# Layer 0 of a two-layer trunk: both product pairs by blocks in thirteen width tiles, two of the four weight sums by accumulating transfers

## The chip, the core and the metric

The kernel runs on one core of a Trainium2 chip. The metric is the device time of one launch in microseconds. The engines are PE (TensorE), DVE (VectorE), ACT (ScalarE), POOL (GpSimd) and SP (SyncE, which here only issues transfers).

## The reference, cut to what matters

Two layers work on 512 prompt tokens and 64 sample tokens, 576 in all (`NT`). Layer 0 is a short gated convolution:

```python
b_gate, c_gate, xa, z = jnp.split(h @ w_in, 4, axis=-1)   # 1024 -> 4 x 2048
u = c_gate * xa
conv, new_buf = causal_dwconv(u, buf, conv_w)
y = b_gate * conv * jax.nn.silu(z)
return y @ w_out, new_buf
```

Layer 1 is an mLSTM block: an input projection to `xm` and `z`, a causal convolution, projections to q, k and v, a chunked recurrence over a matrix state C per head, and an output projection. Both layers start with an RMS norm, and everything is float32.

## The kernel before, in words

**Precision.** A float32 product is made of three fp32r passes. ACT casts a weight tile to `wh`, DVE subtracts to get the rest `wl`; the activations exist as `hi` and `lo`. PE then runs hi*wh, lo*wh and hi*wl.

**Layer 0 by width tiles.** The loop `for f in range(NW)` runs over sixteen tiles of 128 columns of the width 2048. Each tile has four chunks of `w_in`. Chunks 4f and 4f+1 (c gate and x, the *first pair*) end in the buffers `cx` and are computed one tile ahead. Chunks 4f+2 and 4f+3 (b gate and z, the *second pair*) are computed in their own tile; then DVE multiplies them up and splits the result `cv` for the output projection.

**A pair by blocks.** `block_pair` computes two chunks in seven products of half size (Winograd's scheme) instead of eight: each product is 12 matmuls of 128x288, so a pair takes 84 matmuls and not 96. For that the weights of the pair must first be added up. `block_weights` loads two raw tiles `r1`, `r2` of 512 KB (names `wr`), whose halves are a11, a12, a21, a22. DVE makes s1 = a21 + a22 (L297), s2 = s1 + a11 (L298), and later, by `add_up` (L337), s2 += a12 and a21 += a11. The products take a11, s1, s2, a12, a21, the new s2, and a22, in this order; each needs an ACT cast (L263) and a DVE subtract (L264) first. There are four raw buffers, so two pairs; `ws` tiles (s1, s2) come from the pool `X`; `hi`/`lo` weight pairs have four buffers.

The first pair goes by blocks in all tiles after the start. The second pair does so only where `f in SECOND`, which is tiles 3, 5, ..., 13; in the other tiles it is two plain chunks through `raw_weights` and `acc` (L215, L234).

**Order.** Small steps that may run at any time stand in a list `work`, and `run` and `drip` take some of them between products; a second list `slow` holds `query_state`, which multiplies the query by the old state C. The rest is the order of the code, and each engine runs its instructions in that order. SP's queue issues all the loads named here.

**Four places that the change also touches.** `accumulators` opens the PSUM pools; at f = 0 they are opened anew, and `mark` puts four small matmuls behind that. In layer 1, `xm` of each tile is read out of PSUM by DVE (L695). `by_token` transposes k, and its copy `kd` that POOL spreads out (L747), on PE. `query_state` uses tiles `c` of 512 KB, loaded from `cs` into two buffers.

Of the kernel before, what the change touches and what calls it, by code (L numbers as in the profile page):

```python
# [16 lines left out]
P = 128  # L17
# [38 lines left out]
LAG = 6  # L56
AHEAD = 2
FH = 2
SECOND = tuple(range(3, 14, 2))
FI = 1  # L60
EARLY = 3.45
NEARLY = 10
# [5 lines left out]
def trunk(tc, io):  # L68
    nc = tc.nc
    ctx = ExitStack()  # L70
    with ctx:
# [2 lines left out]
        const = ctx.enter_context(tc.tile_pool(name="const", bufs=1))  # L74
        small = ctx.enter_context(tc.tile_pool(name="small", bufs=2))
        accs = [None, None]
        bank_tag = ["b1"]

        def accumulators(name, blocks=None):

            for i in (1,) if blocks is None else (1, 0):
                if accs[i] is not None:
                    accs[i][0].close()
                    accs[i] = None
            for i in (0, 1) if blocks else (1,):
                stack = ctx.enter_context(ExitStack())
                accs[i] = stack, stack.enter_context(tc.tile_pool(name=f"{name}{i}", bufs=4, space=PSUM))
# [56 lines left out]
        load = nc.sync.dma_start  # L144
        store = nc.sync.dma_start
        store_act = nc.scalar.dma_start

        cols = const.tile([P, NCOL], F32, name="cols")
        cst = const.tile([P, NCST], F32, name="cst")
# [150 lines left out]

        def block_weights(c1, c2, six=False):

            groups, behind = [], []
            for i in range(1 + six):
                r1, r2 = weight_tile(), weight_tile()
                for r, c_ in ((r1, c1 + i), (r2, c2 + i)):
                    latest[0] = load(out=r, in_=io["wts"][c_]).ins
                groups.append(block_sums(r1, r2, (8, 4)[i]))
                behind = [r1, r2] if i else []
            ahead_of[c1, c2] = groups, behind  # L310

        def block_pair(c1, c2, fs, xs, out1, out2, add, mid=None, then=None, pops=0, groups=None,
                       behind=()):

            if groups is None:
                groups, behind = ahead_of.pop((c1, c2))
            a11, a12, a21, a22, s1, s2 = range(6)
            fs = [fs[0:4], fs[4:6]]  # L320
            o11, o12, o21, o22 = out1[:, 0:HT], out1[:, HT:NT], out2[:, 0:HT], out2[:, HT:NT]
            pu = X(name="pu")
            p, u = pu[:, 0:HT], pu[:, HT:NT]
            tt = nc.vector.tensor_tensor

            def product(bank_, block_, form, start):
                ws = [parts_of(g[block_]) for g in groups]
                for n, (w, g) in enumerate(zip(ws, fs)):
                    for j, forms_ in enumerate(g):
                        hi, lo = forms_[form]  # L330
                        for i, (a, x) in enumerate(((w[0], hi), (w[0], lo), (w[1], hi))):
                            nc.tensor.matmul(bank_, a[:, j, :], x, start=(start and n + j + i == 0),  # L332
                                             stop=(n == len(groups) - 1 and j == len(g) - 1 and i == 2), skip_group_check=True)

            def add_up(out, block_):
                for g in groups:
                    tt(g[out], g[out], g[block_], ALU.add)  # L337

            bx = block("p1")
            product(bx, a11, "b11", True)  # L340
            by = block("p6")
            nc.scalar.activation(by, bx, AF.Copy, scale=-1.0)  # L342
            run(pops)
            bw = block("p5")
            product(bw, s1, "t1", True)
            m5 = X(HT, name="m5")
            nc.scalar.copy(m5, bw)
            run(pops)
            product(by, s2, "t2", False)
            nc.scalar.copy(u, by)  # L350
            add_up(s2, a12)
            product(bx, a12, "b21", False)
            add_up(a21, a11)
            run(pops)
            if pops:
                drip()
            product(by, a21, "t3", False)
            if xs is None or add:
                nc.scalar.copy(p, by)
            else:  # L360
                bv = block("p7")
                nc.scalar.copy(bv, by)
            product(bw, s2, "b22", False)
            run(pops)
            product(by, a22, "t4", False)
            run(pops)
            mid = list(mid or ())
            for go in mid[0:2]:
                go()
            wx = [parts_of(r[:, 4:8, :]) for r in behind]  # L370
            if then:
                block_weights(*then)
            if add:
                tt(p, p, m5, ALU.subtract)
                tt(o22, o22, p, ALU.add)
                tt(o12, o12, u, ALU.subtract)
                tt(o12, o12, bw, ALU.add)
                tt(o11, o11, bx, ALU.add)
                tt(o21, o21, by, ALU.add)
                return  # L380
            if xs is None:
                tt(o22, p, m5, ALU.subtract)
                nc.scalar.copy(o11, bx)
                tt(o12, bw, u, ALU.subtract)
                nc.scalar.copy(o21, by)
                return
            plain(bx, bw, c1 + 1, xs, None, wx[0:1])
            nc.scalar.copy(o11, bx)
            if mid:
                nc.scalar.copy(o12, bw)  # L390
            tt(o12, o12 if mid else bw, u, ALU.subtract)
            for go in mid[2:3]:
                go()
            if pops:
                drip()
            plain(by, bv, c2 + 1, xs, None, wx[1:2])
            nc.scalar.copy(o21, by)
            if mid:
                nc.scalar.copy(o22, bv)
            tt(o22, o22 if mid else bv, m5, ALU.subtract)  # L400
            for go in mid[3:]:
                go()
# [115 lines left out]
                ins = nc.tensor.matmul(b[:, 0:256], warm[:, 0:128], warm, start=True, stop=True).ins  # L518
            return ins

        accumulators("acc0", False)
        load_buffers("raw", "raw0", 4)
        load_buffers("C", "scratch0")
        layer0[0] = True
# [65 lines left out]
        for f in range(NW):  # L590
# [24 lines left out]
            if f == 0:  # L615
                for i in range(2):
                    acc = mm("acc")
                    products(acc, weights(4 + i), h1, True, True)
                    nc.scalar.copy(cx[i], flat(acc))
                    if i:  # L620
                        block_weights(8, 9)
                    first_blocks(2 + i)
                accumulators("acc0a", True)
                bank_tag[0] = "blk"
                mark(h1[0][0][:, 0:P], h1[0][0][:, 0:HT])
            elif f + 1 < NW:
                block_pair(4 * f + 4, 4 * f + 5, fs, None, *cx, False, pops=1)
# [55 lines left out]
        for f in range(NW):  # L683
# [4 lines left out]
            if f < 2:  # L688
                u = raws[f]
                nc.vector.tensor_tensor(u, u, rb, ALU.mult)  # L690
            else:
                acc = gemm(80 + f, 1, h2)
                u = T(name="xm")
                if f < NW - 2:
                    nc.vector.tensor_tensor(u, flat(acc), rb, ALU.mult)  # L695
                else:
                    nc.scalar.copy(u, flat(acc))
                    nc.vector.tensor_tensor(u, u, rb, ALU.mult)
# [45 lines left out]
        def spread(t, dup):  # L744

            for u in range(2):
                nc.gpsimd.tensor_copy(  # L747
                    dup[:, 128 * u:128 * u + 128].rearrange("p (g s t) -> p g s t", g=4, s=4),
                    t[:, NP + 32 * u:NP + 32 * u + 32].rearrange("p (g t) -> p g t", t=8)
                    .unsqueeze(2).broadcast_to([P, 4, 4, 8]))  # L750
# [140 lines left out]
                h2.append(split(xs[m]))  # L891

        h2 = []
        heads = [dict(h=h, kt=[], qt=[], kd=[], qp=[]) for h in range(NH)]
        order = [4 * h + dt for h in (3, 0, 1, 2) for dt in range(4)]
        for h in (3, 0, 1, 2):
            st = heads[h]
            for dt in range(4):
# [19 lines left out]
                if dt % 2 == 0:  # L918
                    st["kd"].append(T(512, name="kd"))
                dup = st["kd"][-1][:, 256 * (dt % 2):256 * (dt % 2) + 256]  # L920
                spread(k, dup)
                work.append(lambda k=k, dup=dup, h=h, dt=dt: by_token(
                    k, dup, KSCALE, kps[h][dt].rearrange("p (i d) -> p i d", d=128),
                    kss[h][:, :, 128 * dt:128 * dt + 128]))
# [12 lines left out]
            work.append(lambda h=h, t=st["qt"]: gates(8 + h, t))  # L937
            if h == 2:
                break
            work.extend(lambda st=st, dt=dt: scores(st, dt) for dt in range(4))  # L940
            work.extend(lambda st=st, u=u: sample_scores(st, u) for u in range(2))
            if h in (3, 0, 1):
                slow.extend(lambda h=h, i=i: query_state(heads[h], unit(h, *divmod(i, 4)), i) for i in range(8))

        accumulators("acc2", False)
        load_buffers("raw", "raw2", 2)
# [651 lines left out]
def _arrays(a):  # L1598
# [5 lines left out]
    kq = np.stack([_chunks(f["b_w_k"][0]), _chunks(f["b_w_q"][0])], 1)  # L1604
    wts = np.concatenate([t.reshape(-1, P, KD, P) for t in (
        ain, _chunks(f["a_w_out"][0]), bin_[:NW], _chunks(f["b_w_v"][0]), kq, bin_[NW:], _chunks(f["b_w_out"][0]))], 0)
    cols = np.zeros((P, NCOL), np.float32)

    def put(name, v):
# [80 lines left out]
```

## Time and profile before

| | |
|---|---|
| median of 3 runs | 1685.6 us (1679.59 to 1689.01) |
| profiled execution, its own time | 1681.13 us |
| its span, granted TensorE clock | 1679.3 us, 0.992 |
| PE busy | 1646.1 us, 98% |
| DVE busy | 1121.8 us, 67% |
| ACT busy | 780.1 us, 46% |
| POOL busy | 106.8 us, 6% |
| loads `wr` from `wts` | 222 of 512 KB, 3.6 us from issue to landing (median) |

A line of a view names the line of the kernel, the engine, the operation and the tiles, output first. `x2` is the number of instructions put together in a row. In square brackets stands the idle time of the engine just ahead of the row, and who ended it. A row's duration overlaps the next one by some hundredths where an engine is pipelined, so what an instruction costs in a full queue is read from start to start.

### The profile page before, as it was taken

The numbers are of one execution on the slowest core, as the hardware profiler recorded it, in microseconds if no ns is written. First come the engines' busy times: TensorE is split into PE (matmuls) and PEld (weight loads), VectorE is DVE, ScalarE is ACT, GpSimd is POOL, SyncE is SP. The second block draws the span as 40 slices with busy tenths as digits, with TensorE's granted clock in tenths as the row PEclk, the third lists the DMA queues.
The fourth block names the chain that finished last, engine by engine and source line by source line (L and its number), as shares of the span: only waits on it lengthen the run. The fifth ranks groups of instructions, "written<-read, shape, count | busy, mean of one in ns | idle before, by whom it ended". The sixth has DMA issues, their size and how long they took to land. (4 is left out here: it accounts for less than half of the span.)

```text
span 1679.3 us, 31080 instructions
## 1 busy us (share of the span) xinstructions
PE 1646.1 (98%) x12161; PEld 1568.7 (93%) x12161; DVE 1121.8 (67%) x2108; ACT 780.1 (46%) x1546; POOL 106.8 (6%) x241
## 2 busy tenths in 40 slices
PE   9999999999999999999899999999999998999998
PEld 8999999999999999999899989889888887989998
DVE  7988888874336985655956456446458658588775
ACT  5555555543233554434644334344445446556431
POOL 0000000000000000000201010010102000000000
PEclk9999999999999999999999999999999899999999
DMA  5222223233332434535534455454556577998992
GB/s 197 73 94 94 93 93 105 92 101 127 121 122 89 136 123 142 156 116 167 158 101 136 149 176 170 135 172 161 176 182 237 188 239 261 335 332 303 371 332 105
DMA packets 109794, 279.57 MB, mean 166 GB/s; under 512 B 11312, under 2 KB 33712, under 8 KB 109648
## 3 DMA queue, kind: packets, MB, share of 16 engines
q1 hardware_dynamic: 94288, 260.27, 46.4%
q10 hardware_dynamic: 15360, 17.32, 3.0%
q8 instruction: 95, 1.56, 0.4%
q14 instruction: 51, 0.42, 0.1%
HBM read 213.89 MB, written 63.66 MB: 165 GB/s over the span
## 5 line engine op out<-in xcount | busy, mean ns | idle before, releaser
L332 PE MATMUL p<-hi,wh 128*128 128x288 f32 x1316 | 389.0, 297 | 1.2 <-ACT p L342 1.2
L332 PE MATMUL p<-lo,wh 128*128 128x288 f32 x1316 | 386.9, 295 | 0.0
L332 PE MATMUL p<-hi,wl 128*128 128x288 f32 x1316 | 385.9, 295 | 0.0
L234 PE MATMUL acc<-hi,wh 128*128 128x256 f32 (+1 forms) x1328 | 288.5, 298 | 2.1 <-DVE xm L695 1.6
L234 PE MATMUL acc<-lo,wh 128*128 128x256 f32 (+1 forms) x1328 | 287.6, 297 | 0.0
L234 PE MATMUL acc<-hi,wl 128*128 128x256 f32 (+1 forms) x1328 | 287.2, 297 | 0.0
L332 PEld LDWEIGHTS p<-hi,wh 128*128 128x128 f32 x1316 | 246.5, 188 | 14.3 <-issue 3.8
L263 ACT CAST wh<-wr 128x256 fp32r<-128x256 f32 (+1 forms) x266 | 152.0, 572 | 225.4 <-PE p L332 127.1
L332 PEld LDWEIGHTS p<-lo,wh 128*128 128x128 f32 x1316 | 247.1, 188 | 0.0
L332 PEld LDWEIGHTS p<-hi,wl 128*128 128x128 f32 x1316 | 246.3, 188 | 0.0
L214 ACT CAST wh<-wr 128x512 fp32r<-128x512 f32 x202 | 124.8, 620 | 235.9 <-PE acc L234 176.6
L264 DVE TENSOR_TENSOR wl<-wr,wh 128x256 fp32r<-128x256 f32 (+1 forms) x266 | 163.2, 628 | 103.3 <-ACT wh L263 100.2
L234 PEld LDWEIGHTS acc<-hi,wh 128*128 128x128 f32 x1328 | 223.8, 190 | 7.5 <-issue 3.5
L234 PEld LDWEIGHTS acc<-hi,wl 128*128 128x128 f32 x1328 | 223.3, 190 | 1.6 <-issue 1.3
L234 PEld LDWEIGHTS acc<-lo,wh 128*128 128x128 f32 x1328 | 223.3, 190 | 0.5 <-issue 0.2
L215 DVE TENSOR_TENSOR wl<-wr,wh 128x512 fp32r<-128x512 f32 x202 | 138.5, 687 | 110.5 <-ACT wh L214 102.2
L263 ACT CAST wh<-ws 128x512 fp32r<-128x512 f32 (+1 forms) x177 | 99.8, 566 | 205.5 <-PE p L332 112.5
L264 DVE TENSOR_TENSOR wl<-ws,wh 128x512 fp32r<-128x512 f32 (+1 forms) x177 | 108.8, 620 | 58.5 <-ACT wh L263 58.0
L417 PE MATMUL p<-hi,wh 128*128 128x288 f32 x496 | 109.6, 299 | 0.0
L417 PE MATMUL p<-hi,wl 128*128 128x288 f32 x496 | 108.2, 296 | 0.0
L1210 DVE SCALAR_TENSOR_TENSOR c<-c,cols,r 128x512 f32<-128x512 f32 x128 | 91.1, 741 | 23.7 <-PE r L1209 21.2
L417 PE MATMUL p<-lo,wh 128*128 128x288 f32 x496 | 106.9, 295 | 0.0
(382 smaller groups left out, 2572.8 us busy)
## 6 DMA issues: line engine op xcount, KB each, us to landing
wr<-wts SPq DMA_DIRECT2D x222, 512.0 KB, 3.6
c<-cs SPq DMA_DIRECT2D x112, 512.0 KB, 5.9
cs_out<-c SPq DMA_DIRECT2D x64, 512.0 KB, 6.9
x<-xcs SPq DMA_DIRECT2D x20, 288.0 KB, 4.6
x<-xT SPq DMA_DIRECT2D x16, 288.0 KB, 4.1
xcs<-xc ACTq DMA_DIRECT2D x16, 288.0 KB, 2.4
ld<-xcs SPq DMA_DIRECT2D x16, 288.0 KB, 8.6
cp_out<-cp ACTq DMA_DIRECT2D x16, 257.0 KB, 7.5
```

The source lines that it names most:

```text
L214: last_act[0] = nc.scalar.copy(hi, raw[:, 4 * i:4 * i + 4, :]).ins
L215: nc.vector.tensor_tensor(lo, raw[:, 4 * i:4 * i + 4, :], hi.bitcast(F32), ALU.subtract)
L234: nc.tensor.matmul(acc[:, o:o + j - i], a[:, k % 4, :], x[:, i:j], start=(first and k == 0 and p == 0), stop=(last and k == 7 and p == 2))
L263: last_act[0] = nc.scalar.copy(hi, src).ins
L264: nc.vector.tensor_tensor(lo, src, hi.bitcast(F32), ALU.subtract)
L332: nc.tensor.matmul(bank_, a[:, j, :], x, start=(start and n + j + i == 0), stop=(n == len(groups) - 1 and j == len(g) - 1 and i == 2), ski ...
L417: nc.tensor.matmul(b, a[:, k % 4, :], x[:, t:t + HT], start=bool(start) and k == 0 and i == 0, stop=(k == n - 1 and i == 2), skip_group_ch ...
L1210: ins = nc.vector.scalar_tensor_tensor(ct[:, j, :], ct[:, j, :], dec[:, o + j:o + j + 1], r, ALU.mult, ALU.add).ins
```

## The change

The set of tiles whose second pair goes by blocks becomes 2 to 14. In layer 0 two of the four sums of a pair are made by transfers: s1 is loaded from DRAM once more as a21 (256 KB, SP), a transfer issued by POOL adds a22 to it from DRAM, and another adds a11 to a21 in place. DVE keeps s2 = s1 + a11 and s2 += a12. The host stores the chunks concerned with their eight slices permuted. Beside this come four small edits: the PSUM pools of layer 0 are opened in the block form from the start; `xm` of tile 2 of layer 1 goes through a copy by ACT; two empty items stand in `work` ahead of the first `by_token`; and the state tiles `c` are asked for one unit ahead (`meet`).

```diff
-SECOND = tuple(range(3, 14, 2))
+SECOND = tuple(range(2, 15))
...
+        add_load = nc.gpsimd.dma_start
...
         def block_weights(c1, c2, six=False):
 
+            if layer0[0]:
+
+                r1, r2 = weight_tile(), weight_tile()
+                for r, c_ in ((r1, c1), (r2, c2)):
+                    latest[0] = load(out=r, in_=io["wts"][c_]).ins
+                a11, a12, a21, a22 = [r[:, i:i + 4, :] for r in (r1, r2) for i in (0, 4)]
+                s1, s2 = [X(512, name="ws").rearrange("p (k x) -> p k x", x=P) for _ in range(2)]
+                load(out=s1, in_=io["wts"][c2][:, 0:4, :])
+                add_load(out=s1, in_=io["wts"][c2][:, 4:8, :], accum_op=ALU.add)
+                add_load(out=a21, in_=io["wts"][c1][:, 0:4, :], accum_op=ALU.add)
+                nc.vector.tensor_tensor(s2, s1, a11, ALU.add)
+                ahead_of[c1, c2] = [(a11, a12, a21, a22, s1, s2)], []
+                return
...
             add_up(s2, a12)
             product(bx, a12, "b21", False)
-            add_up(a21, a11)
+            if not layer0[0]:
+                add_up(a21, a11)
...
-        accumulators("acc0", False)
+        accumulators("acc0", True)
...
-                accumulators("acc0a", True)
-                bank_tag[0] = "blk"
                 mark(h1[0][0][:, 0:P], h1[0][0][:, 0:HT])
...
-                if f < NW - 2:
+                if 2 < f < NW - 2:
                     nc.vector.tensor_tensor(u, flat(acc), rb, ALU.mult)
...
+        def meet(h, i):
+
+            query_state(heads[h], waiting.pop(), i)
+            n = met.index((h, i)) + 1
+            if n < len(met):
+                waiting.append(unit(met[n][0], *divmod(met[n][1], 4)))
...
+                if (h, dt) == (3, 0):
+                    work.extend([lambda: None] * 2)
...
-                slow.extend(lambda h=h, i=i: query_state(heads[h], unit(h, *divmod(i, 4)), i) for i in range(8))
+                slow.extend(lambda h=h, i=i: meet(h, i) for i in range(8))
...
+    blk = [c for c in range(8, 64) if c % 4 < 2 or c // 4 in SECOND]
+    wts[blk] = wts[blk][:, :, [0, 2, 4, 6, 1, 3, 5, 7]]
```

Over the whole program PE's listing shrinks by 84 matmuls, and POOL's grows by the 54 accumulating transfers of 27 pairs.

DVE before, in an odd tile: the second sum of one pair, then a21 += a11 of the same pair, then the subtracts of the pair ahead of it. Here `wr254`, `wr255` are r1, r2 of the later pair, and `wr239`, `wr240` of the earlier one; `ws` are s1 and s2.

```order
L298 TENSOR_TENSOR ws257_1837<-ws256_1836,wr254_1832 128x512
L337 TENSOR_TENSOR wr255_1833<-wr255_1833,wr254_1832 128x4x128
L264 TENSOR_TENSOR wl267_1886<-ws242_1704,wh267_1885 128x512
L337 TENSOR_TENSOR ws242_1704<-ws242_1704,wr239_1699 128x512
L648 TENSOR_TENSOR cv222_1555<-acc247_1767,cv222_1555 128x576
L264 TENSOR_TENSOR wl268_1904<-wr239_1699,wh268_1903 128x512
L649 TENSOR_TENSOR cv222_1555<-cv222_1555,z243_1707 128x576
L264 TENSOR_TENSOR wl269_1923<-wr240_1700,wh269_1922 128x512
```

DVE after, about one tile: the subtract two rows ahead of the first shown here is the last reader of `wr232`, whose buffer `wr272` takes over; the last row is s2 of the pair that is loaded there, and it needs the accumulated `ws274`.

```order
L265 TENSOR_TENSOR wl265_1811<-wr233_1578,wh265_1810 128x512
L613 TENSOR_TENSOR cx236_1587<-cx236_1587,rb281_505 128x576
L618 TENSOR_TENSOR cv231_1576<-cv231_1576,rb70_470 128x576
L265 TENSOR_TENSOR wl266_1828<-ws235_1582,wh266_1827 128x512
L265 TENSOR_TENSOR wl267_1844<-wr233_1578,wh267_1843 128x512
L265 TENSOR_TENSOR wl280_1888<-wr250_1725,wh280_1887 128x512
L265 TENSOR_TENSOR wl283_1909<-ws252_1729,wh283_1908 128x512
L397 TENSOR_TENSOR b255_1736<-pu256_1737,m5262_1774 128x288
L399 TENSOR_TENSOR z254_1735<-p5260_1757,pu256_1737 128x288
L265 TENSOR_TENSOR wl285_1929<-ws253_1730,wh285_1928 128x512
L659 TENSOR_TENSOR z254_1735<-z254_1735,rb70_470 128x576
L314 TENSOR_TENSOR ws275_1878<-ws274_1877,wr272_1873 128x512
```

Two sums are gone from DVE, and the one that is left (L314) now stands behind two transfers in a row instead of one load.

The queues that feed it. SP after, at the same place (a load of r1, the load of s1 behind it, then r2):

```order
L308 DMA wr272_1873<-wts 128x1024
L311 DMA ws274_1877<-wts 128x512
L308 DMA wr273_1874<-wts 128x1024
L308 DMA wr290_2021<-wts 128x1024
L311 DMA ws292_2025<-wts 128x512
L308 DMA wr291_2022<-wts 128x1024
```

POOL after, at the same place; before, its listing has only the `cpa` copies here:

```order
L312 DMA ws252_1729<-wts 128x512
L617 COPY cpa_507<-u230_1575 128x2
L313 DMA wr251_1726<-wts 128x512
L312 DMA ws274_1877<-wts 128x512
L313 DMA wr273_1874<-wts 128x512
L312 DMA ws292_2025<-wts 128x512
L617 COPY cpa_507<-u270_1871 128x2
L313 DMA wr291_2022<-wts 128x512
```

Two transfers per pair have come onto POOL, in one order with its copies.

PE at the first `by_token`, before (tb is the transpose of the copy kd):

```order
L332 MATMUL p61266_9895<-hi1228_9673,wl1292_10027 128x288
L332 MATMUL p11308_10079<-hl1287_9986,wh1310_10084 128x288
L758 MATMUL tb1313_10109<-cst_70,kd1300_10063 128x128 x2
L332 MATMUL p11308_10079<-hl1287_9986,wh1310_10084 128x288
L332 MATMUL p11308_10079<-hl1287_9986,wl1310_10085 128x288
```

and after:

```order
L346 MATMUL p61329_10045<-hi1291_9823,wl1355_10177 128x288
L346 MATMUL p11371_10229<-hl1350_10136,wh1373_10234 128x288
L771 MATMUL tb1384_10345<-cst_70,kd1363_10213 128x128 x2
L346 MATMUL p11371_10229<-hl1350_10136,wh1373_10234 128x288
L346 MATMUL p11371_10229<-hl1350_10136,wl1373_10235 128x288
```

The transposes stand between the same two matmuls in both, 84 rows earlier in the listing of after, which is as many as the matmuls that went in layer 0.

More of the change, by code (lines that the diff above doesn't have):

```diff
@@ L76, in trunk @@
         accs = [None, None]
-        bank_tag = ["b1"]
+        bank_tag = ["blk"]
         def accumulators(name, blocks=None):
@@ L893, in trunk @@
         h2 = []
+        met = [(h, i) for h in FAR for i in range(8)]
+        waiting = []
+        def meet(h, i):
[3 more added lines that the diff above has]
+                waiting.append(unit(met[n][0], *divmod(met[n][1], 4)))
         heads = [dict(h=h, kt=[], qt=[], kd=[], qp=[]) for h in range(NH)]
@@ L939, in trunk @@
                 break
+            if h == 3:
+                waiting.append(unit(3, 0, 0))
             work.extend(lambda st=st, dt=dt: scores(st, dt) for dt in range(4))
```

## The prediction

> **What bounds the kernel now.** I read the busy shares of the page first, then layer 0 by stretches of two tiles, then PE's waits in the timeline.
>
> ```profile
> PE 1646.1 (98%) x12161; PEld 1568.7 (93%) x12161; DVE 1121.8 (67%) x2108; ACT 780.1 (46%) x1546; POOL 106.8 (6%) x241
> 97.00:143.00 46.00, 46.00 (x349) 46.00 (x349) 38.64 (x68) 24.68 (x49) 1.16 (x2) 1.00 0.32 100
> 189.00:235.00 46.00, 46.00 (x349) 46.00 (x349) 38.91 (x68) 24.62 (x49) 1.17 (x2) 1.00 0.30 99
> 327.00:373.00 46.00, 46.00 (x349) 46.00 (x348) 35.38 (x61) 24.55 (x50) 1.17 (x2) 1.00 0.31 95
> ```
>
> PE is the bound, 98% of the span. The columns of the lower three rows are start and end, length, and the busy time of PE, weight loads, DVE, ACT and POOL, then the granted clock and the share of the transfer engines. In layer 0 PE has no gap: 46.00 of 46.00. So every matmul taken out there is worth its full time, as long as nothing else becomes late. DVE is the nearest, some 39 of 46; ACT has 25.
>
> PE's waits that the four small edits address:
>
> ```profile
> 50.64 0.80 PE L407 MATMUL mark<-hi 128*128 128x288 f32 x4 [1.61 <-ACT cx L619]
> 520.94 0.50 PE L234 MATMUL acc<-hi,wh 128*128 128x256 f32 x2 [1.64 <-DVE xm L695]
> 838.06 0.56 PE L758 MATMUL tb<-cst,kd 128*128 128x128 f32 x2 [3.11 <-POOL kd L747]
> 1003.34 1.07 PE L845 MATMUL qa<-c,qp 128*32 128x512 f32 x8 [0.91 <-DMA c<-cs]
> 1123.03 1.06 PE L845 MATMUL qa<-c,qp 128*32 128x512 f32 x8 [1.05 <-DMA c<-cs]
> 1242.50 1.07 PE L845 MATMUL qa<-c,qp 128*32 128x512 f32 x8 [0.87 <-DMA c<-cs]
> ```
>
> Together 9.2 us. The brackets hold the idle time ahead of the row.
>
> **The matmuls that go.** Seven tiles (2, 4, ..., 14) change from 96 to 84 matmuls in the second pair, so 84 go. What one takes in a full queue:
>
> ```profile
> 1613.27 3.99 PE acc L234 x30
> ```
>
> That is 0.133 us; the stretches above give 46.00/349 = 0.132. 84 x 0.133 = 11.1 us, all on the bound.
>
> **DVE's load.** Its prices are starts in a queue without gaps:
>
> ```profile
> 243.04 0.75 DVE L496 SCALAR_TENSOR_TENSOR cv<-u,cols,cv 128x511 f32<-128x511 f32 x1
> 243.71 0.28 DVE L498 SCALAR_TENSOR_TENSOR cv<-ext,cols,cv 128x64 f32<-128x64 f32 x1
> 243.90 0.68 DVE L264 TENSOR_TENSOR wl<-wr,wh 128x512 fp32r<-128x512 f32 x1
> 244.50 0.74 DVE L496 SCALAR_TENSOR_TENSOR cv<-u,cols,cv 128x510 f32<-128x510 f32 x1
> ```
>
> A 128x512 operation costs 0.60 (243.90 to 244.50), one of 510 to 576 columns 0.67, one of 64 columns 0.19, and one of 288 columns by scale about 0.37. In after, a tile has 14 subtracts and 4 sums (10.8), nine wide operations (6.0), four of 288 (1.5) and the small ones (0.5): 18.8 us. PE's tile becomes 46.15/2 - 0.8 = 22.28 us (two tiles are 348 matmuls now, 336 then, at 0.1326). So DVE stands at 84%. With the four sums that the transfers take over it would be 21.2, 95%. ACT gets three more casts in the even tiles, some 2 us of its 21 idle in 46, and stays clear. The load on DVE alone costs nothing.
>
> **The accumulating transfers.** This is the unknown: no transfer issued by POOL, and none that adds, is in the trace. What it must meet follows from the order. The buffer of r1 comes free at DVE's last subtract on it. Then SP loads r1, s1 behind it, POOL's transfer adds a22, and only then may DVE run s2 (L314). DVE runs in order, so what stands behind L314 waits too: the subtracts for the earlier pair, and with them PE. The rows of the loads:
>
> ```profile
> wr<-wts SPq DMA_DIRECT2D x59, 512.0 KB, 3.5
> DMA to landing us min/median/max: 3.3/3.6/4.8
> 261.55 0.33 SPq L307 DMA_DIRECT2D wr<-wts  x1
> ```
>
> A load of 512 KB takes 3.6 us, and an issue on SP 0.33 us. The s1 load, issued 0.4 behind r1, lands about 0.4 + 3.6 = 4.0 after the subtract that freed the buffer (an estimate; I give 256 KB no discount, since it shares the engines with r1). If the accumulate takes A, s2 may run L = 4.0 + A after that subtract. Between the two DVE has twelve operations, 6.6 us (6.3 for the other kind of pair). A longer L is a stall, once for each pair, twice a tile: DVE then needs 18.8 + 2L - 12.9 per tile, and 0.3 for the gap behind a dependent operation. That meets 22.28 at L = 8.0, so at **A = 4.0 us**. Beyond that each us of A costs 2 us a tile, over tiles 2 to 10 some 18 us, less about 3 us that the prepared weights (two products of twelve matmuls, 1.6 us each) cover once. From tile 11 `cx` shares the pool of `ws`, and the loads come later; I add nothing for it.
>
> What is A? The nearest rows are other transfers of about that size:
>
> ```profile
> xcs<-xc ACTq DMA_DIRECT2D x16, 288.0 KB, 2.4
> cp_out<-cp ACTq DMA_DIRECT2D x16, 257.0 KB, 7.5
> ```
>
> The quickest is 2.4 us, a busy one 7.5; both ends go into the range. An addition reads two tiles of 256 KB, as many bytes as one `wr` load, and I take that row: 3.6 us. It is 0.4 us inside the limit, so I charge nothing, with little left. At 2.4 nothing either; at 7.5 it is 18 x 3.5 - 3 = 60 us. The second accumulate (a21, L313) is needed only at the fifth product, four products or 6.4 us of PE later than s1; it hides behind these. POOL's `cpa` copies (1.17 us in 46) stand in the same queue, but u is done well before.
>
> The Trainium skill, DMA: Bandwidth & Descriptors, "Anatomy of one DMA — SWDGE (gpsimd) path", fits a transfer issued by GpSimd with 2.0 us plus its bytes over 436 GB/s; an estimate by it is 2.6 us for 256 KB, which no run here shows for an adding one. By it L would be 6.6, no wait at all, and the sum the same.
>
> At the start L314 of the first pair stands ahead of the weight subtracts for the first tile:
>
> ```profile
> 22.35 1.29 DVE L215 TENSOR_TENSOR wl<-wr,wh 128x512 fp32r<-128x512 f32 x2
> ```
>
> DVE comes there at 22.35, r1 has landed by about 21.8 (its load is issued at 18.0 in before, plus 3.8), and s1 is loaded ahead of it. Between no wait and 2 us; I take nothing, since PE has weights ahead.
>
> **The four waits.** *mark*: nothing is moved and the reopening, which waits for the last `cx`, goes; the weights of the first products are cast before. 1.6 us. *xm*: the read-out goes from DVE to ACT, where it stands behind these:
>
> ```profile
> 518.54 0.67 ACT L165 CAST hi<-xm 128x576 fp32r<-128x576 f32 x1
> 519.13 0.62 ACT L214 CAST wh<-wr 128x512 fp32r<-128x512 f32 x1
> 520.05 1.41 DVE L695 TENSOR_TENSOR xm<-acc,rb 128x576 f32<-128x576 f32 x2
> ```
>
> ACT's copy runs from about 519.7 to 520.4, where the first of DVE's two ended at about 520.75. PE gains 0.4 of 1.64, between 0 and 1.6. *c*: the groups of `qa` that waited stood 25 rows of PE behind the one before; in after the closest are 37 rows apart, and in before groups 37 and 38 rows apart did not wait. 2.8 us, between 0 and 2.8. *kd*: the transposes did not move on PE, and the copies that they wait for are on POOL as before:
>
> ```profile
> 830.74 7.49 POOL L747 COPY kd<-k 128x128 f32<-128x128 f32 x2 [22.92 <-issue]
> ```
>
> Two copies of 128x128 take 7.49 us there. I take nothing, between 0 and 3.1: the two empty items do not do what they look like.
>
> **The sum.** 11.1 + 1.6 + 0.4 + 2.8 = 15.9 us. From the profiled execution, 1681.1, that is 1665.2. The median of the runs is 4.5 above the profiled one; the forecast for a median is 1685.6 - 15.9 = 1669.7, 1670, with a range of its own of 1664 to 1676.
>
> **The rivals.**
> *The accumulates are late (slower).* A over 5.5 us makes L314 the place where DVE stands, and PE runs out of weights twice a tile. At A = 6 the loss is 18 x 2 - 3 = 33, the time 1685.6 - 15.9 + 33 = 1703. For it: the 7.5 of `cp_out`, and the addition runs beside the 512 KB load of r2, issued meanwhile. It decides from A = (15.9 + 8.4 + 3)/18 + 4 = 5.5. Against it: layer 0 uses only 0.30 of the transfer engines. A second way to the same: DVE shuts POOL out while it works, as the 7.49 us for two `kd` copies suggest, and POOL cannot issue in time.
> The Trainium skill, SBUF — State Buffer, "Who interferes with whom", says that POOL's transfers get their descriptors late while DVE runs operations that use two ports, such as copies; a tensor_tensor with two inputs in SBUF contends only with what GpSimd reads. The `kd` row agrees with the latter part. No run here shows the former.
> *Gains and stalls cancel.* A between 4.6 and 5.5 costs 8 to 24 us: within 8.4 us of before, about 1686 at A = 5.1.
> *All four waits go.* If POOL's `kd` copies happen to run in a freer stretch, 3.1 more: 1666.6.
>
> **How the numbers follow.** No change that can be told is within 0.5%, 8.4 us. Chances: forecast (A up to 4.6, where the loss is under 8 us) 0.50, all four waits 0.07, cancelling 0.17, late 0.26. Faster 0.57, same 0.17, slower 0.26. The range starts at 1660, the four-wait case less the scatter of the runs (6 us below the median), and ends at 1705, A of about 6.2 (18 x 2.2 - 3 = 37, 1706); some 0.15 lies above, 0.03 below.
>
> **What the profile of after would show.** Right: a tile of 22.3 us in layer 0, PE 46 of 46 there, L314 with waits of under 1.5 us each, `mark` and the three `qa` without their waits, `kd` still near 3 us, `xm` near 1.2. Wrong: DVE idle ahead of L314 for 3 us and more, released by POOL's transfer, and PE idle ahead of `p` for `wl` in each tile. The median landing of the `ws` accumulate tells A: 4.0 is the limit.

## The result: slower by 0.66%

| | before | after |
|---|---|---|
| median of 7 runs | 1684.77 us | 1696.69 us |
| ratio, 95% interval | | 1.0066 (1.0049 to 1.0084) |
| profiled execution, own time | 1681.13 us | 1696.83 us |
| its span, clock | 1679.3 us, 0.992 | 1695.0 us, 0.988 |

Forecast was 1670 with 0.57 for faster; what came is the place and the mechanism of the rival *the accumulates are late*, at 0.26, but not its condition: it asked for an accumulate of over 5.5 us, and the median here is 4.4. The ratio says some 11 us more; the two profiled executions stand 15.7 apart, since that of before is one of its quickest runs.

Layer 0 after, in stretches of two tiles; the columns are start and end, length, busy time of PE, weight loads, DVE, ACT and POOL, the clock and the share of the transfer engines:

```profile
97.00:143.00 46.00, 43.33 (x317) 41.86 (x316) 37.67 (x67) 26.30 (x55) 7.13 (x9) 1.00 0.63 155
143.00:189.00 46.00, 40.43 (x297) 39.26 (x296) 33.13 (x61) 25.43 (x53) 7.36 (x10) 1.00 0.60 144
189.00:235.00 46.00, 45.39 (x326) 44.45 (x325) 36.81 (x64) 27.13 (x56) 7.57 (x10) 0.96 0.64 161
327.00:373.00 46.00, 44.28 (x327) 43.12 (x326) 36.19 (x66) 26.82 (x57) 8.15 (x10) 1.00 0.64 154
```

PE, which had 46.00 of 46.00 and 349 matmuls, now has gaps and runs 297 to 327. DVE is not full, it stands: 33 to 38 us. The transfer engines went from 0.30 to 0.62. What ended the longest waits of DVE and of PE in layer 0 (us, times, longest):

```profile
DVE ws L314 <- DMA ws<-wts: 49.3, 24, 4.1
PE p L346 <- DVE wl L265: 14.8, 14, 3.0
```

DVE waits at L314 for the transfer that adds, 24 times for 2.05 us, and PE waits for the `wl` that stand behind. One such pair, SP's rows first, then POOL, DVE and PE:

```profile
151.43 0.33 SPq L308 DMA_DIRECT2D wr<-wts  x1
151.81 0.43 SPq L311 DMA_DIRECT2D ws<-wts  x1
156.41 0.89 POOL L312 DMA_DIRECT2D ws<-wts  x1 [8.70 <-DVE u L614]
160.87 0.69 DVE L314 TENSOR_TENSOR ws<-ws,wr 128x512 f32<-128x512 f32 x1 [2.60 <-DMA ws<-wts]
162.22 0.40 PE L346 MATMUL p<-hi,wl 128*128 128x288 f32 x1 [2.01 <-DVE wl L265]
```

From the issue of r1 to s2 are 9.44 us: 0.38 to the issue of s1, 4.60 to the issue of the accumulate, 4.46 to s2. (The releaser in POOL's bracket is not the last one: the u it names was long there; it is the landing of s1.) The transfers after, KB each, median us to landing:

```profile
ws<-wts SPq DMA_DIRECT2D x27, 256.0 KB, 3.9
ws<-wts POOLq DMA_DIRECT2D x27, 256.0 KB, 4.4
wr<-wts POOLq DMA_DIRECT2D x27, 256.0 KB, 4.0
```

How much layer 0 lost is read from one line of each kernel, the first and the last start of the product that ends a tile (count, duration, first and last start). Before, then after:

```profile
L649 DVE TENSOR_TENSOR cv<-cv,z x16: 750/750/759, 64.5 to 390.2; 128x576 f32<-128x576 f32 x16
L662 DVE TENSOR_TENSOR cv<-cv,z x16: 747/750/758, 63.5 to 405.0; 128x576 f32<-128x576 f32 x16
```

14.8 us later where 11.1 less were due. Against the kernel *s2 written later* (below), which has the same transfers and no such loss, it is 27.3 us. Not all of that is idle time: after two of PE's longest waits, of 3.01 and 2.25 us, the granted clock fell for a while (the column before the last two):

```profile
188.00:192.00 4.00, 4.00 (x21) 4.00 (x21) 4.00 (x9) 0.62 (x1) 0.00 (x0) 0.61 0.20 18
260.00:264.00 4.00, 3.20 (x13) 3.20 (x14) 4.00 (x9) 0.62 (x1) 0.00 (x0) 0.57 0.25 44
```

There the matmuls start 0.24 us apart and not 0.13. Added up from start to start, some 17 us of the loss lie in fourteen waits of PE, some 3 in these two slow stretches, and some 7 in many starts that are a few tenths late. The four small waits, where they are now, after:

```profile
48.12 0.69 PE L422 MATMUL mark<-hi 128*128 128x288 f32 x4
534.49 0.53 PE L235 MATMUL acc<-hi,wh 128*128 128x256 f32 x2 [1.04 <-ACT xm L710]
839.37 0.40 PE L346 MATMUL p<-hi,wh 128*128 128x288 f32 x1 [2.80 <-ACT p L356]
846.57 1.25 POOL L760 COPY kd<-k 128x128 f32<-128x128 f32 x2 [25.16 <-issue]
```

`mark` and the `qa` no longer wait. The wait for `kd` is not there, but a little ahead of it PE now waits 2.80 for another step, and after that the two `kd` copies took 1.25 us and not 7.49.

### The profile page after: what moved, and what is told of

Read it like the earlier page. It is cut to its first block, busy times and chain, and to the rows that moved or that the text cites. A ratio compares the mean times of both kernels' runs of the same rounds, so it can differ in the third digit from the quotient of the medians.

```text
span 1695.0 us, 31248 instructions
## 1 busy us (share of the span) xinstructions
PE 1650.9 (97%) x12077; PEld 1564.0 (92%) x12077; DVE 1118.6 (66%) x2117; ACT 802.8 (47%) x1610; POOL 148.0 (9%) x295
## 5 line engine op out<-in xcount | busy, mean ns | idle before, releaser
L346 PE MATMUL p<-hi,wl 128*128 128x288 f32 x1512 | 446.7, 298 | 15.1 <-DVE wl L265 14.8
L346 PE MATMUL p<-hi,wh 128*128 128x288 f32 x1512 | 448.4, 298 | 4.2 <-ACT p L356 2.8
L346 PE MATMUL p<-lo,wh 128*128 128x288 f32 x1512 | 446.4, 296 | 0.0
L264 ACT CAST wh<-wr 128x512 fp32r<-128x512 f32 (+1 forms) x294 | 169.5, 576 | 210.4 <-PE p L346 120.7
L235 PE MATMUL acc<-hi,wh 128*128 128x256 f32 (+1 forms) x1104 | 240.2, 298 | 2.1 <-ACT xm L710 1.0
L265 DVE TENSOR_TENSOR wl<-wr,wh 128x512 fp32r<-128x512 f32 (+1 forms) x294 | 180.2, 632 | 89.5 <-ACT wh L264 88.8
L235 PE MATMUL acc<-hi,wl 128*128 128x256 f32 (+1 forms) x1104 | 239.0, 297 | 0.0
L235 PE MATMUL acc<-lo,wh 128*128 128x256 f32 (+1 forms) x1104 | 238.3, 297 | 0.0
L264 ACT CAST wh<-ws 128x512 fp32r<-128x512 f32 x198 | 112.7, 570 | 225.9 <-PE p L346 123.4
L265 DVE TENSOR_TENSOR wl<-ws,wh 128x512 fp32r<-128x512 f32 x198 | 122.7, 625 | 51.0 <-ACT wh L264 50.6
L432 PE MATMUL p<-hi,wh 128*128 128x288 f32 x496 | 109.2, 300 | 0.0
L432 PE MATMUL p<-hi,wl 128*128 128x288 f32 x496 | 107.3, 295 | 0.0
L432 PE MATMUL p<-lo,wh 128*128 128x288 f32 x496 | 107.0, 295 | 0.0
```

What stands on the lines that cost most here:

```text
L235: nc.tensor.matmul(acc[:, o:o + j - i], a[:, k % 4, :], x[:, i:j], start=(first and k == 0 and p == 0), stop=(last and k == 7 and p == 2))
L264: last_act[0] = nc.scalar.copy(hi, src).ins
L265: nc.vector.tensor_tensor(lo, src, hi.bitcast(F32), ALU.subtract)
L432: nc.tensor.matmul(b, a[:, k % 4, :], x[:, t:t + HT], start=bool(start) and k == 0 and i == 0, stop=(k == n - 1 and i == 2), skip_group_ch ...
```

## The experiments

The theory after the result: what costs is where s2 stands in DVE's order, twelve operations behind the subtract that frees the raw buffer, while load, load and accumulate take 9.4 us. The rivals: the traffic of the transfers or POOL's part in it; DVE or the raw buffers being unfit for blocks in both pairs; the small edits. All ratios are to the kernel before.

| kernel | ratio (95%) | last `cv<-cv,z` |
|---|---|---|
| after | 1.0066 (1.0049 to 1.0084) | 405.0 |
| small edits alone | 0.9991 (0.9980 to 1.0001) | 390.3 |
| four sums on DVE | 0.9913 (0.9894 to 0.9931) | 378.4 |
| a21 alone by transfer | 0.9918 (0.9900 to 0.9936) | 379.5 |
| s1 alone by transfers | 1.0033 (1.0021 to 1.0045) | 398.0 |
| s1 asked for earlier | 1.0008 (0.9996 to 1.0021) | 395.2 |
| s2 written later | 0.9906 (0.9887 to 0.9926) | 377.7 |
| transfer copies, does not add | 0.9966 (0.9954 to 0.9977) | 384.6 |
| four sums, kd on DVE | 0.9904 (0.9887 to 0.9920) | 377.9 |
| before with tiles 2 to 14 | 0.9960 (0.9943 to 0.9978) | 378.5 |
| after with tiles 3, 5, ..., 13 | 1.0017 (1.0001 to 1.0033) | 393.1 |

### The small edits alone

```diff
# before, with the four small edits only
-        accumulators("acc0", False)
+        accumulators("acc0", True)
...
```

> The kernel before with the four small edits alone; products and sums as before. Theory (the loss of the change lies in layer 0 alone, at the sum that waits for an accumulate): all that PE no longer waits for at mark (1.6), kd (3.1), the three qa (2.8) and part of xm (0.6) is gained, 8.1 us, ratio 0.995, and layer 0 stays without a gap in PE. Rival (part of the loss comes from these edits, for instance from what moved behind kd or the earlier loads of c): ratio 1.000 or more, with new waits of PE after 600 us.

0.9991 and not 0.995: most of the 8 us did not come. `mark` comes 1.0 us earlier, but eight microseconds on PE waits for the next late step, and the wait for `kd` stayed, as the order had it (the kernel's own rows):

```profile
57.30 0.40 PE L332 MATMUL p<-hi,wh 128*128 128x288 f32 x1 [0.61 <-ACT m L347]
PE tb L756 <- POOL kd L745: 3.1, 1, 3.1
```

The last `cv<-cv,z` is where it was, 390.3. From the first `qa` to the first `r` PE needs 390.6 us and not 394.0, and 390.6 to 390.8 in every later kernel with that edit: 3.4 us. With `xm`, 0.6, that makes 4; the ratio holds 0 to 3.4. Most of the difference is the clock. After the wait for `kd` the granted clock was 0.55 from 836 to 840 us and 0.60 from 840 to 844 in this profiled execution, and 1.00 after the same wait in that of before. From the first `r` to the end, which these edits don't touch, before took 366.0 us and this kernel 373.6 (the others 367.5 to 374.0). The trace has half the clock for some 27 us of that in before and for some 40 here, which by estimate is 6.6 of the 7.6 us. Over all executions of this experiment the mean granted clock was 0.989 here and 0.991 in before, which is some 3 us of 1683. Why it is lower is not shown.

### Four sums on DVE

```diff
-                load(out=s1, in_=io["wts"][c2][:, 0:4, :])
-                add_load(out=s1, in_=io["wts"][c2][:, 4:8, :], accum_op=ALU.add)
-                add_load(out=a21, in_=io["wts"][c1][:, 0:4, :], accum_op=ALU.add)
+                nc.vector.tensor_tensor(s1, a21, a22, ALU.add)
...
-            if not layer0[0]:
-                add_up(a21, a11)
+            add_up(a21, a11)
```

> The changed kernel with all four weight sums on DVE again, no accumulating transfer: both pairs by blocks in tiles 2 to 14. Theory (only the wait for the accumulate costs): DVE has 21.2 us of work in a tile of 22.28, PE stays without gaps in layer 0, 84 matmuls less are worth 11.1 us and the waits 8.1: ratio 0.9886, some 1666 us. Rival A (DVE was full, so that the transfers were needed): 95 per cent plus gaps for dependent operations is more than PE's tile, PE loses 0.5 to 1 us a tile, 6 to 13 us, ratio 0.992 to 0.996. Rival B (four raw buffers cannot feed seven half products in both pairs, whoever adds): about as slow as the changed kernel, 1.005.

0.9913. The same stretch of two tiles as above:

```profile
143.00:189.00 46.00, 46.00 (x350) 46.00 (x349) 44.69 (x80) 29.19 (x61) 1.17 (x2) 1.00 0.31 92
```

DVE is at 44.69 of 46 and PE has no gap. Rivals A and B fall: DVE at 97% by its rows feeds PE, and the accumulating transfers were not needed. The 0.9886 of the theory is missed all the same, because it counted 8.1 us for the small edits. Blocks in both pairs are worth 378.4 against 390.2 us, 11.8.

### One sum by transfer

```diff
# a21 alone: s1 made by DVE
-                load(out=s1, in_=io["wts"][c2][:, 0:4, :])
-                add_load(out=s1, in_=io["wts"][c2][:, 4:8, :], accum_op=ALU.add)
+                nc.vector.tensor_tensor(s1, a21, a22, ALU.add)
```

> The changed kernel with only the sum a21 += a11 made by a transfer; s1 is made by DVE from the two loaded tiles. Theory: the chain of load, load and accumulate ahead of s2 is gone, the other accumulate is needed four products later and hides; DVE 20.0 of 22.28; no gap in PE: ratio 0.9886 as with four sums, or better than these if DVE is short there. Rival (any accumulating transfer, by its traffic or by POOL, slows the loads or DVE): between 0.995 and 1.006.

```diff
# s1 alone: a21 += a11 made by DVE
-                add_load(out=a21, in_=io["wts"][c1][:, 0:4, :], accum_op=ALU.add)
...
-            if not layer0[0]:
-                add_up(a21, a11)
+            add_up(a21, a11)
```

> The changed kernel with only s1 made by transfers; a21 += a11 is DVE's again. Theory: the chain ahead of s2 is as long as in the changed kernel, about 9.5 us from the load of r1 to s2, and DVE has 0.6 us more in a tile: as slow as the changed kernel or slower, ratio 1.006 to 1.012. Rival (the traffic of the transfers): half of the accumulates are gone, half of the loss of 28 us goes, ratio about 0.998.

0.9918 and 1.0033. An accumulate that nobody waits for early is free: with a21 alone PE is at 46.00 and the transfer engines at 0.46. With s1 alone, at the same 0.46, PE loses again:

```profile
143.00:189.00 46.00, 46.00 (x350) 46.00 (x349) 42.60 (x75) 29.75 (x62) 4.63 (x7) 1.00 0.46 115
143.00:189.00 46.00, 42.79 (x313) 41.39 (x312) 37.29 (x67) 25.01 (x53) 4.30 (x6) 1.00 0.46 124
```

The traffic is the same in both, and only one loses, so it isn't the traffic. With s1 alone the loss is smaller than the theory said: 1.0033 lies between its 1.006 and the rival's 0.998, and against four sums on DVE layer 0 loses 19.6 us (398.0 against 378.4) where after loses 26.6. Two things differ. The accumulate is somewhat quicker without the one on a21 beside it, 4.0 us and not 4.3 (median between 100 and 300 us). And with a21 += a11 on DVE again mostly 12 or 13 of its operations stand between the issue of r1 and s2, and not 10 or 11. How much of the 7 us belongs to each is not shown.

### s1 asked for earlier

```diff
+                n = turns.index(c1) + 1
+                if n < EARLY_SUMS:
+                    early[turns[n]] = first_sum(turns[n] + 1, T)
                 nc.vector.tensor_tensor(s2, s1, a11, ALU.add)
```

(`first_sum` holds the load of s1 and the accumulate, `turns` the order of the pairs.)

> The changed kernel, but the load of s1 and the accumulate on it are asked for one pair ahead, into tiles of another pool, for the first eighteen of 27 pairs; the same transfers and the same sums. Theory (DVE stands at s2 because r1's free buffer, the load of s1 and the accumulate follow one another, 9.5 us): the accumulate has landed before r1 has, s2 waits for r1 alone, under 1 us; of the 28 us that PE loses in layer 0 the 23 or so of these tiles go: ratio 0.991 to 0.994. Rival (the traffic of the transfers, or POOL's work, slows DVE, ACT or the loads): the same transfers, ratio still 1.004 to 1.008.

1.0008, a miss of both. Where it did what it should, between 97 and 235 us, PE is nearly whole; at the start, and from where the early asking ends, it is not:

```profile
51.00:97.00 46.00, 42.39 (x312) 41.19 (x311) 35.95 (x65) 22.97 (x46) 6.28 (x9) 1.00 0.53 131
97.00:143.00 46.00, 45.31 (x341) 44.84 (x340) 38.82 (x68) 28.46 (x59) 8.17 (x10) 1.00 0.68 170
143.00:189.00 46.00, 45.59 (x345) 45.35 (x344) 38.95 (x69) 28.63 (x59) 8.17 (x10) 1.00 0.66 163
235.00:281.00 46.00, 42.60 (x318) 41.90 (x317) 37.69 (x67) 27.02 (x57) 6.94 (x9) 1.00 0.56 135
```

The rows that do well have the most traffic, 0.66 to 0.68, which speaks against the rival again. But s2 also moved in DVE's order: in one pair of two it stands 3 to 5 operations behind the issue of r1, in the other 18 to 22. So this run moves two things.

### s2 written later

```diff
-                nc.vector.tensor_tensor(s2, s1, a11, ALU.add)
                 ahead_of[c1, c2] = [(a11, a12, a21, a22, s1, s2)], []
...
             product(bx, a11, "b11", True)
+            if layer0[0]:
+                for g in groups:
+                    tt(g[s2], g[s1], g[a11], ALU.add)
```

> The changed kernel with one line moved: s2 = s1 + a11 is written behind the first product of its own pair and not where the pair is loaded, so that on DVE it stands some eighteen operations behind the subtract that frees the buffer (10.5 us) and not twelve (6.6). Theory (the chain is as long as before, but what costs is DVE's order): the chain of 9.5 us fits, DVE does not stand, ratio 0.991 to 0.994. Rival A (the transfers as such): 1.004 to 1.008. Rival B (s2 now comes too late for the third product): the wait turns up on PE ahead of p, ratio above 1.

0.9906. This is the run that decides: every transfer of the changed kernel is in it, two for each pair on POOL, and the whole loss is gone. One pair, SP, POOL and DVE (L356 is s2 here):

```profile
154.23 0.33 SPq L308 DMA_DIRECT2D wr<-wts  x1
154.61 0.43 SPq L311 DMA_DIRECT2D ws<-wts  x1
159.10 0.86 POOL L312 DMA_DIRECT2D ws<-wts  x1 [7.22 <-DMA ws<-wts]
167.88 0.68 DVE L356 TENSOR_TENSOR ws<-ws,wr 128x512 f32<-128x512 f32 x1
143.00:189.00 46.00, 46.00 (x350) 46.00 (x349) 40.17 (x71) 29.69 (x62) 7.53 (x10) 1.00 0.71 166
```

s2 comes 13.65 us after the issue of r1 and waits for nothing. The accumulate is even slower than in after (4.7 us against 4.3, same stretch), the transfer engines are at 0.71, and PE is whole.

### The addition priced

```diff
-                add_load(out=s1, in_=io["wts"][c2][:, 4:8, :], accum_op=ALU.add)
+                add_load(out=s1, in_=io["wts"][c2][:, 4:8, :])
```

> The changed kernel with the transfer on s1 copying a22 over it and not adding it (so s1 leaves a21 out); every instruction and every wait stands as in the changed kernel. It prices the addition: Theory (what counts is the chain, with its fixed parts): issue to landing 4.0 to 4.4 us as with the addition, the time within 0.2 per cent of the changed kernel, ratio 1.006. Rival (the addition, which must read what it adds to, is what makes the transfer slow): 2.4 to 3.4 us, the chain 1 to 2 us shorter, 18 us less for each: ratio 0.985 to 0.996.

0.9966: the rival is right here. A plain copy by the same queue lands after 3.3 us (median between 100 and 300 us), the addition takes 4.3. (s1 then lacks a21; the kernel leaves that sum out.) The order of every engine is that of after, so this is a measured dose: the chain from the issue of r1 to s2 takes 8.68 us and not 9.44 (medians between 90 and 295 us), and the last `cv<-cv,z` comes 20.4 us earlier (384.6 against 405.0). The forecast's price, 18 us for each microsecond, was for tiles 2 to 10. These tiles take 14.8 us less here for 0.76 us of chain, and some 3 of the 14.8 are the two slow stretches of after, which this run does not have: 16 to 19 us for each.

```profile
145.49 0.33 SPq L308 DMA_DIRECT2D wr<-wts  x1
150.39 0.55 POOL L312 DMA_DIRECT2D ws<-wts  x1 [7.58 <-DVE u L614]
153.73 0.69 DVE L314 TENSOR_TENSOR ws<-ws,wr 128x512 f32<-128x512 f32 x1 [1.40 <-DMA ws<-wts]
```

### kd on DVE

```diff
# four sums on DVE, and
-                spread(k, dup)
-                if (h, dt) == (3, 0):
-                    work.extend([lambda: None] * 2)
+                spread(k, dup, nc.vector.tensor_copy if (h, dt) == (3, 0) else nc.gpsimd.tensor_copy)
```

> The variant with four sums on DVE, and the two copies kd of the first by_token on DVE instead of POOL, without the two empty items. Theory: the two copies took 7.49 us on POOL while DVE was busy and PE waited 3.1 us for them; on DVE they take some 0.4 and the wait goes: 0.9913 - 0.0018 = 0.9895. Rival (another wait is next, as behind mark): 0.991.

0.9904 against 0.9913: the intervals overlap, so the 3 us are not shown by the times. In the trace the wait for `kd` is gone and from the first `tb` to the first `qa` PE needs 293.7 us, where the variant with four sums alone needs 295.8. With *s2 written later* it is the quickest of the study, 16 us under before.

### The parts of the change by themselves

```diff
# before
-SECOND = tuple(range(3, 14, 2))
+SECOND = tuple(range(2, 15))
```

> The kernel before with the set of tiles whose second pair goes by blocks set to 2 to 14, and nothing else: four sums on DVE, the four small edits undone. Theory: 84 matmuls less at 0.1327 us are 11.1 us, all on the bound, and layer 0 stays without gaps: ratio 0.9934. The difference to the variant with four sums and the small edits (0.9913) is what these are worth, some 3 us, not 9. Rival (DVE's 95 per cent needs the start that the edit at mark gives): 0.996 or more.

0.9960, the rival's number, and the theory's 0.9934 lies outside the interval; but the rival's reason is not it: in layer 0 the whole gain is there (378.5 against 390.2, 11.7 us). It is given back later. The three `qa` waits, 2.8 us in before, are

```profile
PE qa L845 <- DMA c<-cs: 5.9, 3, 3.8
```

in the profiled execution, one of them 3.8, and from the first `qa` to the first `r` PE needs 399.4 us and not 394.0. Of these 5.4 us 3.1 are the waits; after the one of 3.8 the granted clock was 0.50 between 1113 and 1118 us. In these two profiles, then, the edit on `c` is worth more beside the blocks than alone.

```diff
# after
-SECOND = tuple(range(2, 15))
+SECOND = tuple(range(3, 14, 2))
```

> The changed kernel with the set of tiles as before (3, 5, ..., 13), so that the even tiles run two plain chunks between the pairs; transfers and small edits as in the changed kernel, 20 pairs instead of 27. Theory: the chain of some 9.5 us is met by more DVE and PE work between two pairs, and DVE has 34 us of work in 46 plus some 9 of standing: PE loses under 3 us, ratio 0.998 to 1.002 (the small edits alone gave 0.9991). Rival (each accumulated pair costs about 1 us whatever the tile): 20 pairs cost 20 us, ratio 1.011.

1.0017, as the theory had it: with plain chunks between the pairs the same late sums cost almost nothing, though the accumulate takes 5.5 us here (median).

```profile
DVE ws L314 <- DMA ws<-wts: 37.5, 16, 5.3
```

DVE stands 37.5 us at L314 in 16 waits, and PE has 46.00 of 46.00 between 143 and 189 us. 20 pairs at 1 us each would have been 1.011. The last `cv<-cv,z` is at 393.1, 2.8 us behind the small edits alone.

## Why the prediction was wrong, point by point

**The matmuls that go: right.** 84 x 0.133 = 11.1 us; without a gap layer 0 ends 11.7 us earlier.

**DVE's load alone costs nothing: right,** and more than was claimed: with all four sums it still feeds PE.

**What the accumulate must meet: right.** The limit of 8.0 us from the subtract to s2, and 18 us for each microsecond beyond, came from DVE's order. Over tiles 2 to 10 that formula gives 18 x 1.4 - 3 = 22 us for the chain of after and 18 x 0.7 - 3 = 9.6 for that of the plain copy; against *s2 written later* these tiles lost 21.4 and 6.6. Some 3 of the 21.4 are the two stretches at a lower clock, for which the formula has no term.

**What it takes: wrong, and this is the step that failed.** "I take that row: 3.6 us. It is 0.4 us inside the limit". The chain was put at 4.0 + 3.6 = 7.6 us and is 9.4 (median of 17 pairs between 90 and 295 us). Three terms: s1 lands 4.3 us after the issue of r1 (0.3 more); between that landing and POOL's issue pass 0.67 us, a term that the sum did not have; the accumulate takes 4.3 (0.7 more); medians do not add up exactly. No single one would have done it: with 4.3 for the accumulate and the rest as forecast the formula gives 18 x 0.3 - 3 = 2.4 us. The row taken for the price was a load on another queue that adds nothing; of the copy on POOL's queue 3.3 us were measured, so the addition is 1.0 of it. An estimate by the fit in the Trainium skill, DMA: Bandwidth & Descriptors, "Anatomy of one DMA — SWDGE (gpsimd) path", is 2.6 us; the runs have 3.3 for the copy and medians of 4.0 to 5.5 with the addition.

**Two places put at nothing.** "I take nothing" at the start and "I add nothing for it" from tile 11: layer 0 of after lost 27.3 us in all, 2.0 by the end of tile 1 and 3.9 behind tile 10. There the load of s1 is issued 1.6 to 2.7 us behind that of r1, and the chain takes 10.6 to 12.8 us.

**The rival had the mechanism and the place, but not the cause of the size.** It laid everything on the accumulate, from 5.5 us up, and that took 4.3; more than half of what the chain took beyond 7.6 came by the terms ahead of it. The waits at L314 came out between the two signs that were named: 2.05 us on average, where under 1.5 meant right and 3 and more meant wrong. The rival was given 0.26 where the limit and the estimate stood 0.4 us apart on a slope of 18. With a price known only between 2.4 and 7.5 that margin was no reason for 0.57 on the other side.

**The second way of that rival: not seen.** POOL's issues of the accumulate all took 0.86 to 1.2 us, also where DVE was busy with operations on two tiles, as in *s2 written later*. What passes between issue and landing the trace does not split.

**The four waits.** 4.8 us were forecast, and the trace shows 4: `qa` 3.4 (2.8 forecast), `xm` 0.6 (0.4), `mark` nothing, not 1.6, since what it gains is lost again at the wait eight microseconds later; `kd` nothing, as forecast from the order. Its disappearance in after is an exchange: PE waits 2.80 us shortly before for a product whose weights came late, and arrives at `kd` when the copies are done.

**Where the change's 11 us come from:** 11.7 gained by the blocks, 4 by the small edits, 27 lost through the stand at L314, the 3 us of lower clock among them.

## What to carry to other kernels

A transfer that takes a sum off a busy engine helps only if the instruction that needs it stands far enough behind in that engine's order; count the operations between the event that starts the chain and the one that waits, and compare the sum of them with the whole chain, hand-overs included. When such a margin comes out at a few tenths and its loss repeats in every tile, move the waiting instruction (one line here, 27 us) or first try whether the transfer is needed at all. A small wait that is removed is a gain only when the next late step is known: one of four came back here, and one never went.

## What the runs showed of the hardware

- A transfer of 256 KB on POOL's queue lands 3.3 us after its issue when it copies s1 and 4.0 to 5.5 when it adds to it (medians of the runs; what sets the difference between the runs is not shown); its issue holds POOL 0.55 and 0.87 us (medians):

```profile
L312 POOL DMA_DIRECT2D ws<-wts x26: 546/553/644, 55.3 to 346.1; - x26
L312 POOL DMA_DIRECT2D ws<-wts x26: 859/868/1214, 55.3 to 364.9; - x26
```

- From the landing of s1 to POOL's next issue pass 0.67 us, from the landing of the accumulate to DVE's start 0.02.
- Two POOL copies of 128x128 took 7.49 us in one kernel and 1.25 in another, with the same neighbours in the order and DVE busy with operations on two tiles in both; what decides is not shown.
- In layer 0 of after, PE's waits of 3.01 and 2.25 us were followed by 3.4 us each at half the granted clock, and waits of 1.68 and 2.01 us were not. It is not a fixed rule: the wait of 3.1 us for `kd` was followed by such a stretch in *the small edits alone* and not in before.
